# MLP of a two-layer diffusion transformer: layer 1's modulation summed in PSUM, late row sums on GpSimd, and another order of the second stage's first loads and splits

## The chip, the core and the metric

The kernel runs on one core of a Trainium2 chip. The core's engines are TensorE (PE; its weight loads are listed as PEld), VectorE (DVE), ScalarE (ACT), GpSimd (POOL) and SyncE (SP), which here issues the DMA transfers. SBUF is the working memory, PSUM the eight banks into which PE writes products. The metric is the device time of one execution in microseconds (us).

## The reference

Two layers, each an adaptive norm, a token mixer and an MLP, over 1024 tokens of 1024 channels; layer 0 also carries 256 context tokens. What matters here is the MLP and the modulation that scales its input:

```python
mod_l = (jax.nn.silu(c) @ ada_w[layer] + ada_b[layer]).reshape(batch, 1, N_MOD, D_MODEL)
mod_c = (jax.nn.silu(c_ctx) @ ada_w[layer] + ada_b[layer]).reshape(1, 1, N_MOD, D_MODEL)
...
def modulate(x, g, mod, i):
    return rms_norm(x, g) * (1 + mod[:, :, i + 1]) + mod[:, :, i]

def sq_relu_mlp(h, w1, w2):
    return jnp.square(jax.nn.relu(h @ w1)) @ w2
...
x = x + mod_l[:, :, 5] * sq_relu_mlp(modulate(x, norm2_g[layer], mod_l, 3), mlp_w1[layer], mlp_w2[layer])
```

`w1` is 1024 x 4096, `w2` 4096 x 1024, all in float32. The modulation of a layer is a vector times a 1024 x 6144 matrix, once for the tokens and once for the context.

## The kernel before

**Arithmetic.** A float32 product is made of three TensorE products of a high and a low part. So each operand is split: ACT rounds it to its high part (L389), GpSimd or DVE subtracts that to get the low part (L390).

**The MLP's first stage** (`mlp_hidden`) makes the hidden layer in 16 pairs of 2 x 128 hidden channels, as a seven-product scheme for 2 x 2 blocks. `start` does pairs 0 and 1, `pair` the pairs 2 to 15, each with the products "11", "S1", "12", "S2", "22", "S3", "S4" of 12 matmuls of 128 x 512; in layer 0 two direct products of the context (24 matmuls of 128 x 256 each) stand after "12" and after "S3". Every product takes the next PSUM bank of a ring `A`: in layer 0 after `start` the seven banks 4, 5, 6, 0, 1, 2, 3, in layer 1 all eight. Bank 7 (`N`) takes the small sums of the modulation in layer 0. A bank is emptied ("drained") by ACT (L800 for "11", L592 for the context), by DVE (L635) for the rest. ACT then does relu and square (L592, L593), and the blocks of the hidden layer are stored to DRAM (`hd`, `hc`; L595).

**Sums for the second stage.** For each pair three column sums and two row sums of its hidden blocks are also made on DVE and stored (`kept_sum`, L609 to L611). For pairs 0 and 1, whose blocks are complete too early for that, `late_load` fetches four blocks from DRAM after pairs 7 and 10 (L617), and the "late sums" are made in the next pair.

**Operands.** While pair b runs, the generator `sums(b + 1)` makes the next pair's operands, a step after each product: additions on GpSimd (L553) and splits (ACT L389, GpSimd L390). In pair 15 the generator `ahead` takes that place: it loads (L915), adds (L960) and splits the first operands of the second stage.

**The filler.** In layer 0 the first stage also makes layer 1's modulation (`ada_sums`): 12 blocks of 512 columns, each of eight loads of 128 x 512 (L204) that DVE multiplies, row by row, by the entries of silu(c) and adds to the sum so far (L211 for the first, L213 for the rest); the first four blocks do this for tokens and context ("two streams"), the rest for the tokens alone. PE then adds up over the 128 partitions with tiny matmuls by ones (L222), and DVE adds the bias (L225). `fill` advances this by one step at three places of a pair. The sums lie in SBUF tiles `acc`, of which there is one per stream (512 columns for the tokens, two of 256 for the context).

**The second stage** (`mlp_out`) multiplies the hidden blocks by `w2`; its first products are those of line L1037.

**Order.** PE, DVE, ACT and GpSimd run `start` in program order, and with SP also pairs 14 and 15; elsewhere a scheduler orders each engine's instructions. Every engine's queue runs in order.

Of the kernel before, what the change touches and what calls it, by code (L numbers as in the profile page):

```python
# [14 lines left out]
ALU = mybir.AluOpType  # L15
# [6 lines left out]
ND = D // P  # L22
# [24 lines left out]
PG = 1024  # L47
# [32 lines left out]
def cuts(big, n, *offs):  # L80
    return [big[:, o : o + n] for o in offs]
# [15 lines left out]
class Kernel:  # L97
# [99 lines left out]
    def ada_sums(self, layer, block, streams, tp, psp, tag):  # L197


        nc, a = self.nc, self.a  # L200
        acc = [[tp.tile([P, n], F32, tag=f"acc{v}") for _ in range(512 // n)] for v, n in enumerate((512, 256)[:streams])]
        for k in range(ND):
            w = tp.tile([P, 512], F32, tag="raw")
            nc.sync.dma_start(w, a["ada_w"][layer, k * P : (k + 1) * P, block * 512 : block * 512 + 512])  # L204
            for v in range(streams):
                c = self.cs[:, k, v : v + 1]
                n = 512 // len(acc[v])
                for i, t in enumerate(acc[v]):
                    x = w[:, i * n : i * n + n]
                    if k == 0:  # L210
                        nc.vector.tensor_scalar(t, x, c, None, op0=ALU.mult)  # L211
                    else:
                        nc.vector.scalar_tensor_tensor(t, x, c, t, op0=ALU.mult, op1=ALU.add)  # L213
            if k % 4 == 3:
                yield
        pt = psp.tile(tag, "adapt")
        for v in range(streams):
            n = 4 // len(acc[v])
            for i in range(4):
                o = 8 * v + 2 * i  # L220
                t = acc[v][i // n][:, i % n * P : i % n * P + P]
                nc.tensor.matmul(pt[:, o : o + 2], t, self.ones[:, 0:2], start=True, stop=True)  # L222
        c0 = block * 4
        for v in range(streams):
            nc.vector.tensor_tensor(  # L225
                self.mod[layer][:, c0 : c0 + 4, v], pt[:, 8 * v : 8 * v + 8].rearrange("p (i e) -> p i e", e=2)[:, :, 0],
                self.v(V_AB + layer * 48 + c0, 4), op=ALU.add,
            )
        yield
# [276 lines left out]
    def mlp_hidden(self, layer, groups, hds, begin, slots, tp, feed, filler):  # L506
# [4 lines left out]
        nc, a = self.nc, self.a  # L511
        F, W = self.F, self.W
        ctx = groups[2:]
        c0, c1 = (slice(t0, t0 + n) for t0, n, _ in LGS)
        psp = self.banks(A=(0, 1, 2, 3, 4, 5), N=(7, 6) if ctx else (6, 7))
        parts = [W[i][:, o : o + PG] for i in slots[:5] for o in (PG, 0)]
# [11 lines left out]
        x = self.x  # L528
# [6 lines left out]
        def op(src):  # L535
            o = tp.tile([P, PG], F32R, tag="op")
            o = o[:, :H], o[:, H:]
            self.split(*o, src, nc.gpsimd)
            return o
# [8 lines left out]

        def sums(b, A, w):

            a11, a12, a21, a22 = w
            s = tp.tile([P, H], F32, tag="s")
            add = lambda o, p, q, how: nc.gpsimd.tensor_tensor(o, p, q, op=how)  # L553
            A["11"] = op(a11)
            add(s, a21, a22, ALU.add)
            yield
            A["S1"] = op(s)
            add(s, s, a11, ALU.subtract)
            yield
            A["12"] = op(a12)  # L560
            yield
            A["S2"] = op(s)
            add(a11, a11, a21, ALU.subtract)
            yield
            A["22"] = op(a22)
            add(s, a12, s, ALU.subtract)
            yield
            A["S3"] = op(a11)
            yield
            A["S4"] = op(s)  # L570
            yield
            if ctx:
                A["21"] = op(a21)
            yield
# [12 lines left out]
        def temp(n=512):  # L587
            return tp.tile([P, n], F32, tag="u")
# [8 lines left out]
        def part(b, i):  # L597
            return hd[b][:, i * H : i * H + H]
# [7 lines left out]
            job = lambda: finish(ps, tp.tile([P, CTX], F32, tag=tag), hc[b][:, e * CTX : e * CTX + CTX])  # L606
            job() if later is None else later.append(job)

        def kept_sum(b, i, o, p, q, how=ALU.add):  # L609
            tt(o, p, q, how)  # L610
            nc.sync.dma_start(part(b, i), o)  # L611

        def late_load(b):

            h = [temp() for _ in range(4)]
            for t, i in zip(h, (5, 7, 8, 2)):
                nc.sync.dma_start(t, part(b, i))  # L617

            def late_sums():
                column_sums(b, h[0], h[2], h[3])  # L620
                row_sums(b, h[0], h[1], h[3])

            return late_sums

        def column_sums(b, h11, h21, h22):
            kept_sum(b, 1, temp(), h21, h11, ALU.subtract)
            kept_sum(b, 0, temp(), h11, h22)
            kept_sum(b, 4, h21, h21, h22)

        def row_sums(b, h11, h12, h22):  # L630
            kept_sum(b, 6, temp(), h12, h22, ALU.subtract)
            kept_sum(b, 3, h12, h11, h12)

        def tt(o, p, q, how=ALU.add):
            nc.vector.tensor_tensor(o, p, q, op=how)  # L635
# [150 lines left out]
        def pair(b, A, nxt):  # L786
# [58 lines left out]
            step()  # L845
            step()
            pending["row"] = lambda: row_sums(b, h11, v, h22)

        def ahead():


            at = tp.tags["op"][1]
            w = W[slots[5]]
            tp.place("op", [parts[(at + i) % 10] for i in range(10)] + [w[:, :PG], w[:, PG:]])
            tp.place("raw", cuts(F, PG, 0, PG, 2 * PG))
            tp.place("b", cuts(F, PG, 5 * PG, 6 * PG))
            eng = nc.gpsimd
            if filler:
                yield
                yield  # L860
            for k in range(2):
                feed.load(k)
            feed.load_a(2)
            yield
            feed.split_a(0, eng)
            yield
            feed.split_b(0, eng)
            feed.load_b(2)
            yield
            if not filler:  # L870
                yield
                yield
            for k in (1, 2):
                feed.split_a(k, eng)
                feed.split_b(k, eng)
                yield

        R, pending = {}, {}
        E = mybir.EngineType
# [1 line left out]
        def load(b):  # L881
            if b < NFF // 2 and b not in R:
                R[b] = raws(b)

        A = start()
        for b in range(2, NFF // 2):
            B = {}
            for i in range(1, 2 if ctx else 3):
                load(b + i)
            nxt = sums(b + 1, B, R[b + 1]) if b + 1 < NFF // 2 else ahead()  # L890
            if b < NFF // 2 - 2:
                pair(b, A, nxt)
            else:
                with self.tc.manual_schedule(engines={E.PE, E.DVE, E.Activation, E.Pool, E.SP}):
                    pair(b, A, nxt)
            A = B
            if b in (7, 10, NFF // 2 - 1):
                pending.pop("row")()
                if b < 11:
                    pending["late"] = late_load((b - 7) // 3)  # L900
# [1515 lines left out]
```

## Time and profile before

| | us |
|---|---|
| median of 3 runs | 2829.03 (2823.62 to 2830.92) |
| profiled execution | 2817.14 |
| its span in the trace | 2815.4, mean granted clock 0.989 |
| PE busy | 2711.1 (96%) |
| DVE busy | 1955.4 (69%) |
| ACT busy | 1474.7 (52%) |
| POOL busy | 1116.1 (40%) |
| layer 0's pairs 2 to 15 | 822 to 1229.3 |

The trace is of one execution and has its own time, beside the median of several. A row of waits reads: the engine, what it wrote and its line, what it waited for, then the total in us, the number of waits, and the longest. In a timeline the columns are the start, the length, the engine, line, operation, output <- input, shape and count, and in brackets the idle time before it and what ended it.

### The profile page before, as it was taken

To read this page: it belongs to the slowest core of one execution; us is meant where nothing else is said; L and a number is where in the kernel's file an instruction comes from. 1 tells how busy PE (TensorE), PEld (TensorE's weight loads), DVE (VectorE), ACT (ScalarE), POOL (GpSimd) and SP (SyncE) were. 2 spreads that over 40 slices of the span, in tenths; PEclk is the share of its full clock that TensorE was granted. 3 is DMA by queue.
4 is the path that set the end of the run, shared out by engine and by line. 5 is a ranking of instruction groups with operands and counts; after the bars stand their busy time and mean duration, and the time that the engine had idled before them with its cause. 6 is when DMAs were issued, how large, how long until landed. Compare 5 with 4: busy or idle time off the path is not lost.

```text
span 2815.4 us, 40957 instructions
## 1 busy us (share of the span) xinstructions
PE 2711.1 (96%) x14747; PEld 2299.1 (82%) x14747; DVE 1955.4 (69%) x3300; ACT 1474.7 (52%) x2611; POOL 1116.1 (40%) x740
## 2 busy tenths in 40 slices
PE   6899999999999999989999999999999999999999
PEld 3788888878788787868888889999988888878887
DVE  4646555578877977666777756888884667666776
ACT  4655554544664243434346646888775555444442
POOL 3521121111238565640001345777776398740000
PEclk9999999999999999989999999999999999999999
DMA  7222224442324566578855820000036245478674
GB/s 238 67 78 94 97 100 135 143 161 87 119 85 151 172 223 226 175 243 303 288 191 177 260 79 24 24 20 27 24 110 218 70 165 195 169 260 278 220 235 153
DMA packets 194662, 428.36 MB, mean 152 GB/s; under 512 B 21129, under 2 KB 47337, under 8 KB 194457
## 3 DMA queue, kind: packets, MB, share of 16 engines
q1 hardware_dynamic: 194456, 425.73, 45.4%
q8 instruction: 116, 1.90, 0.3%
q14 instruction: 90, 0.73, 0.1%
HBM read 322.90 MB, written 102.74 MB: 151 GB/s over the span
## 4 chain that ended last, share of the span: by engine, by line
PE 63%; DVE 12%; DMA 8%; issue 4%; ACT 3%; POOL 1%; SPq 0%; DVEq 0%; POOLq 0%; ACTq 0%
PE psum L580 17%; PE psum L1037 12%; DMA hhiraw<-in_w 5%; PE psum L415 4%; PE psum L417 4%; PE psum L416 4%; PE psum L2004 4%; PE psum L2190 3%; PE psum L1133 3%; PE psum L1910 3%; DVE W L390 2%; DVE F L635 1%; DVE F L213 1%; POOL W L390 1%; DMA hd<-F 1%
## 5 line engine op out<-in xcount | busy, mean ns | idle before, releaser
L390 POOL TENSOR_TENSOR W<-F,W 128x512 fp32r<-128x512 f32 (+2 forms) x323 | 518.7, 1621 | 544.0 <-ACT W L389 433.0
L1037 PE MATMUL psum<-W,W 128*128 128x512 f32 x2688 | 616.7, 392 | 13.1 <-POOL W L390 8.0
L1037 PEld LDWEIGHTS psum<-W,W 128*128 128x128 f32 x2688 | 505.8, 189 | 123.7 <-POOL W L390 10.1
L580 PE MATMUL psum<-hhi,W 128*128 128x512 f32 (+1 forms) x1600 | 451.0, 362 | 8.4 <-DVE x L635 6.5
L389 ACT ACTIVATE W<-F 128x512 fp32r<-128x512 f32 (+2 forms) x380 | 273.4, 739 | 261.4 <-POOL F L553 93.8
L580 PEld LDWEIGHTS psum<-hhi,W 128*128 128x128 f32 x1600 | 291.6, 194 | 54.3 <-DVE x L635 5.6
L580 PE MATMUL psum<-hlo,W 128*128 128x512 f32 (+1 forms) x800 | 288.3, 360 | 0.0
L389 ACT ACTIVATE W<-hhiraw 128x1024 fp32r<-128x1024 f32 x98 | 104.0, 1061 | 307.8 <-PE psum L1037 203.4
L415 PE MATMUL psum<-hhi,W 128*128 128x512 f32 (+1 forms) x624 | 232.7, 373 | 0.5 <-ACT F L1422 0.5
L417 PE MATMUL psum<-hhi,W 128*128 128x512 f32 (+1 forms) x624 | 226.6, 363 | 0.0
L416 PE MATMUL psum<-hlo,W 128*128 128x512 f32 (+1 forms) x624 | 226.2, 362 | 0.0
L553 POOL TENSOR_TENSOR F<-F 128x512 f32<-128x512 f32 x112 | 168.7, 1507 | 20.2 <-DMA F<-in_w 10.5
L960 DVE TENSOR_TENSOR hhiraw<-hhiraw 128x512 f32<-128x512 f32 x154 | 106.4, 701 | 96.7 <-DMA hhiraw<-in_w 95.9
L580 PEld LDWEIGHTS psum<-hlo,W 128*128 128x128 f32 x800 | 155.1, 194 | 21.3 <-issue 0.2
L390 DVE TENSOR_TENSOR W<-hhiraw,W 128x1024 fp32r<-128x1024 f32 x98 | 119.7, 1222 | 63.3 <-ACT W L389 62.0
L382 POOL TENSOR_TENSOR hlo<-F,hhi 128x512 fp32r<-128x512 f32 (+1 forms) x24 | 27.4, 1144 | 341.5 <-ACT F L373 341.5
L415 PEld LDWEIGHTS psum<-hhi,W 128*128 128x128 f32 x624 | 118.0, 189 | 20.9 <-ACT x L389 2.5
L416 PEld LDWEIGHTS psum<-hlo,W 128*128 128x128 f32 x624 | 118.1, 189 | 17.1 <-issue 2.2
L417 PEld LDWEIGHTS psum<-hhi,W 128*128 128x128 f32 x624 | 117.9, 189 | 16.7 <-issue 0.2
L592 ACT ACTIVATE F<-F 128x512 f32<-128x512 f32 x82 | 51.3, 626 | 141.5 <-DVE F L635 141.5
L390 DVE TENSOR_TENSOR W<-hloraw,W 128x1024 fp32r<-128x1024 f32 x98 | 121.0, 1234 | 4.1 <-ACT W L389 4.1
L580 PE MATMUL psum<-x,W 128*128 128x512 f32 x504 | 123.5, 390 | 0.0
(442 smaller groups left out, 6363.4 us busy)
## 6 DMA issues: line engine op xcount, KB each, us to landing
F<-in_w SPq DMA_DIRECT2D x104, 512.0 KB
hloraw<-hd SPq DMA_DIRECT2D x90, 512.0 KB
hhiraw<-in_w SPq DMA_DIRECT2D x72, 512.0 KB
hd<-F SPq DMA_DIRECT2D x142, 256.0 KB
hhiraw<-in_w SPq DMA_DIRECT2D x116, 256.0 KB
F<-in_ada_w SPq DMA_DIRECT2D x96, 256.0 KB
hd<-x SPq DMA_DIRECT2D x90, 256.0 KB
F<-in_win SPq DMA_DIRECT2D x33, 512.0 KB
```

Of the source, the lines that this page charges most:

```text
L389: nc.scalar.activation(hi, src, AF.Copy)
L390: eng.tensor_tensor(lo, src, hi.bitcast(F32), op=ALU.subtract)
L415: nc.tensor.matmul(ps, sh, mh, start=i == 0, stop=False)
L416: nc.tensor.matmul(ps, sh, ml, start=False, stop=False)
L417: nc.tensor.matmul(ps, sl, mh, start=False, stop=i == n - 1)
L553: add = lambda o, p, q, how: nc.gpsimd.tensor_tensor(o, p, q, op=how)
L580: nc.tensor.matmul(ps, w[i][:, p], B[j][k], start=first and j == 0 and m == 0, stop=last and j == 3 and m == 2)
L960: tt = lambda o, p, q, how: eng.tensor_tensor(o, p, q, op=how)
L1037: nc.tensor.matmul(bank(base + i), A[u][:, p], B[v], start=first and m == 0, stop=last and m == 2)
L1133: nc.tensor.matmul(bank(k), B[u][:, i * P : i * P + P], A[v][:, half], start=f == 0 and m == 0, stop=f == NFF - 1 and m == 2,)
L1910: nc.tensor.matmul(ps, s[:, c], m[:, j, t0 : t0 + QT], start=j == 0 and i == 0, stop=j == ND - 1 and i == 2)
L2004: nc.tensor.matmul(u.o[:, :QT], v[x], p[y], start=c == 0 and m == 0, stop=c == 2 * NB - 1 and m == 2)
```

## The change

Four things are changed, all in the MLP's code.

The modulation's sums grow in PSUM. `ada_sums` takes a bank for each stream (`X`, `Y`); the first product of a block (now L209) and the six additions behind it (L211) go there, and only the eighth addition (L216) writes to the SBUF tile `acc` that PE reads. In layer 0, after `start`, the ring `A` has the banks 0 to 4, `Y` bank 5, `X` bank 6, `N` bank 7.

The row sums of the late sums run on GpSimd; column sums stay on DVE.

`ahead` has another order in both layers: the first weight load and the second step's weights come first, the splits of step 0 each a step earlier in layer 0, the second step's splits before the third's.

The raw tiles of `ahead` are taken in the order 2PG, 0, PG in place of 0, PG, 2PG.

```diff
@@ ada_sums
+        sums = [psp.tile(t, "adacc") for t in "XY"[:streams]]
         acc = [[tp.tile([P, n], F32, tag=f"acc{v}") for _ in range(512 // n)] for v, n in enumerate((512, 256)[:streams])]
...
-                n = 512 // len(acc[v])
-                for i, t in enumerate(acc[v]):
-                    x = w[:, i * n : i * n + n]
-                    if k == 0:
-                        nc.vector.tensor_scalar(t, x, c, None, op0=ALU.mult)
-                    else:
-                        nc.vector.scalar_tensor_tensor(t, x, c, t, op0=ALU.mult, op1=ALU.add)
+                if k == 0:
+                    nc.vector.tensor_scalar(sums[v], w, c, None, op0=ALU.mult)
+                elif k < ND - 1:
+                    nc.vector.scalar_tensor_tensor(sums[v], w, c, sums[v], op0=ALU.mult, op1=ALU.add)
+                else:
+                    n = 512 // len(acc[v])
+                    for i, t in enumerate(acc[v]):
+                        x = slice(i * n, i * n + n)
+                        nc.vector.scalar_tensor_tensor(t, w[:, x], c, sums[v][:, x], op0=ALU.mult, op1=ALU.add)
@@ mlp_hidden
-        def kept_sum(b, i, o, p, q, how=ALU.add):
-            tt(o, p, q, how)
+        def kept_sum(b, i, o, p, q, how=ALU.add, eng=nc.vector):
+            eng.tensor_tensor(o, p, q, op=how)
...
-                row_sums(b, h[0], h[1], h[3])
+                row_sums(b, h[0], h[1], h[3], nc.gpsimd)
...
-        def row_sums(b, h11, h12, h22):
-            kept_sum(b, 6, temp(), h12, h22, ALU.subtract)
-            kept_sum(b, 3, h12, h11, h12)
+        def row_sums(b, h11, h12, h22, eng=nc.vector):
+            kept_sum(b, 6, temp(), h12, h22, ALU.subtract, eng)
+            kept_sum(b, 3, h12, h11, h12, ALU.add, eng)
@@ ahead
-            tp.place("raw", cuts(F, PG, 0, PG, 2 * PG))
+            tp.place("raw", cuts(F, PG, 2 * PG, 0, PG))
...
-            if filler:
-                yield
-                yield
-            for k in range(2):
-                feed.load(k)
+            feed.load(0)
+            feed.load_a(1)
+            yield
+            feed.split_a(0, eng)
+            yield
+            feed.split_b(0, eng)
             feed.load_a(2)
             yield
-            feed.split_a(0, eng)
-            yield
-            feed.split_b(0, eng)
+            feed.load_b(1)
+            feed.split_a(1, eng)
+            yield
             feed.load_b(2)
             yield
-            if not filler:
-                yield
-                yield
-            for k in (1, 2):
-                feed.split_a(k, eng)
-                feed.split_b(k, eng)
-                yield
+            feed.split_b(1, eng)
+            yield
+            feed.split_a(2, eng)
+            feed.split_b(2, eng)
+            yield
@@ before the loop over the pairs 2 to 15
+        if ctx:
+            psp.tags.update(self.banks(A=(0, 1, 2, 3, 4), N=(7,), X=(6,), Y=(5,)).tags)
```

How the instructions stand, at three places. The first is DVE at the bias addition of the modulation's first block (L225, now L228), in a pair early in layer 0's first stage; `cs` holds silu(c), the `F` and `x_` tiles without psum are SBUF. Before:

```order
L225 TENSOR_TENSOR mod_83<-psum,vec 128x4 x2
L211 TENSOR_SCALAR F<-F,cs 128x512
L211 TENSOR_SCALAR x_7126<-F,cs 128x256
L211 TENSOR_SCALAR x_7127<-F,cs 128x256
L213 SCALAR_TENSOR_TENSOR F<-F,cs 128x512
L213 SCALAR_TENSOR_TENSOR x_7126<-F,cs,x_7126 128x256
L213 SCALAR_TENSOR_TENSOR x_7127<-F,cs,x_7127 128x256
```

The same place of the changed kernel:

```order
L228 TENSOR_TENSOR mod_83<-psum,vec 128x4 x2
L216 SCALAR_TENSOR_TENSOR F<-F,cs,psum 128x512
L216 SCALAR_TENSOR_TENSOR x_7126<-F,cs,psum 128x256
L216 SCALAR_TENSOR_TENSOR x_7127<-F,cs,psum 128x256
L209 TENSOR_SCALAR psum<-F,cs 128x512 x2
L211 SCALAR_TENSOR_TENSOR psum<-F,cs,psum 128x512 x3
L638 TENSOR_TENSOR x_7126<-psum,x_7126 128x512
```

Before, the second block's sum begins behind the first block's bias addition; in the changed order the second block's last step stands there, and behind it the third block begins.

The second place is SP near the end of layer 0's first stage, where the second stage's first loads stand (L915, now L919; `in_w` is `w2`, `hd_0` pair 0's hidden blocks). Before, from the last sums of pair 14 on:

```order
L611 DMA hd_14_6492<-x_7127 128x512 x3
L1110 DMA x_10153<-xs_116 128x512
L1110 DMA x_10154<-xs_116 128x512
L1110 DMA x_10155<-xs_116 128x512
L1110 DMA x_10153<-xs_116 128x512
L595 DMA hd_15_6493<-x_7127 128x512
L595 DMA hc_15_6509<-F 128x256
L915 DMA F<-in_w 128x512 x2
L915 DMA F<-hd_0_6478 128x1024
L915 DMA F<-in_w 128x512 x2
L915 DMA F<-hd_1_6479 128x1024
```

The changed kernel has the first `L919 DMA F<-in_w 128x512 x2` among the stores of pair 13 and goes on like this from the sums of pair 14:

```order
L919 DMA F<-hd_0_6478 128x1024
L919 DMA F<-in_w 128x512 x2
L614 DMA hd_14_6492<-x_7127 128x512 x2
L1114 DMA x_10125<-xs_116 128x512
L1114 DMA x_10126<-xs_116 128x512
L1114 DMA x_10127<-xs_116 128x512
L1114 DMA x_10129<-xs_116 128x512
L1114 DMA x_10130<-xs_116 128x512
L598 DMA hd_15_6493<-x_7127 128x512
L598 DMA hc_15_6509<-F 128x256
L919 DMA F<-in_w 128x512 x2
L919 DMA F<-hd_1_6479 128x1024
```

Step 0's loads and step 1's weights have moved ahead of pair 15's stores; the hidden tiles of steps 1 and 2 still stand behind the first of them (step 2's comes right after the last row). The loads of L1114 are tiles of `x` for the second stage's end.

The third place is GpSimd there: the last pair's additions (L553, now L556), and the second stage's (L960, now L964). Before:

```order
L553 TENSOR_TENSOR F<-F 128x512
L390 TENSOR_TENSOR W_4597<-F,W_4597 128x512
L553 TENSOR_TENSOR F<-F 128x512
L390 TENSOR_TENSOR W_4597<-F,W_4597 128x512
L390 TENSOR_TENSOR W_4594<-F,W_4594 128x512 x2
L960 TENSOR_TENSOR F<-F 128x512
L390 TENSOR_TENSOR W_4596<-F,W_4596 128x1024
```

Now:

```order
L964 TENSOR_TENSOR F<-F 128x512
L393 TENSOR_TENSOR W_105<-F,W_105 128x512
L556 TENSOR_TENSOR F<-F 128x512
L393 TENSOR_TENSOR W_105<-F,W_105 128x512
L556 TENSOR_TENSOR F<-F 128x512
L393 TENSOR_TENSOR W_106<-F,W_106 128x512 x2
L556 TENSOR_TENSOR F<-F 128x512
L393 TENSOR_TENSOR W_4597<-F,W_4597 128x512
L556 TENSOR_TENSOR F<-F 128x512
L393 TENSOR_TENSOR W_4596<-F,W_4596 128x1024
L393 TENSOR_TENSOR W_4597<-F,W_4597 128x512
L393 TENSOR_TENSOR W_4594<-F,W_4594 128x512 x2
```

The second stage's first addition stands ahead of all the last pair's operands, and the split of its first weights (W_4596, 128x1024) ahead of that pair's last three.

More of the change, by code (lines that the diff above doesn't have):

```diff
@@ L854, in ahead @@
             tp.place("op", [parts[(at + i) % 10] for i in range(10)] + [w[:, :PG], w[:, PG:]])
-            tp.place("raw", cuts(F, PG, 0, PG, 2 * PG))
+            tp.place("raw", cuts(F, PG, 2 * PG, 0, PG))
             tp.place("b", cuts(F, PG, 5 * PG, 6 * PG))
             eng = nc.gpsimd
-            if filler:
-                yield
-                yield
-            for k in range(2):
-                feed.load(k)
-            feed.load_a(2)
+            feed.load(0)
+            feed.load_a(1)
             yield
@@ L867, in ahead @@
             feed.split_b(0, eng)
+            feed.load_a(2)
+            yield
+            feed.load_b(1)
+            feed.split_a(1, eng)
+            yield
             feed.load_b(2)
             yield
-            if not filler:
-                yield
-                yield
-            for k in (1, 2):
-                feed.split_a(k, eng)
-                feed.split_b(k, eng)
-                yield
+            feed.split_b(1, eng)
[3 more added lines that the diff above has]
+            yield
         R, pending = {}, {}
```

## The prediction

> **What bounds the kernel now.** I read the chain of waits first, by engine, then the waits inside layer 0's first MLP stage (822 to 1229 us, where the modulation's sums run beside it), then windows and single waits of that stage, and last the two places where a second stage begins.
>
> ```profile
> PE 63%; DVE 12%; DMA 8%; issue 4%; ACT 3%; POOL 1%; SPq 0%; DVEq 0%; POOLq 0%; ACTq 0%
> 822.00:1229.30 407.30, 392.19 (x2094) 340.27 (x2092) 315.48 (x387) 158.53 (x308) 251.22 (x169) 0.97 0.55 181
> 1015.00:1041.00 26.00, 26.00 (x142) 22.28 (x141) 21.98 (x24) 8.68 (x16) 16.89 (x12) 1.00 0.70 233
> ```
>
> TensorE (PE) holds most of the chain. The windows give us, busy us of PE, weight load, DVE, ACT and POOL, then PE's granted clock. In this stage PE is busy for 392.2 of 407.3 us at a mean clock of 0.97. At full clock the work is 392.2 x 0.97 = 380 us, as the third row shows it is done where nothing is late (26 us of work in 26 us, clock 1.00). So at most 407.3 - 380 = 27 us can be won in the stage. Where they are lost:
>
> ```profile
> PE psum L222 <- DVE F L213: 7.7, 4, 3.7
> PE psum L580 <- DVE x L635: 6.5, 4, 3.1
> PE psum L580 <- ACT F L800: 1.0, 1, 1.0
> DVE x L635 <- PE psum L580: 4.0, 1, 4.0
> ACT F L592 <- DVE F L635: 104.6, 21, 12.2
> POOL W L390 <- ACT W L389: 133.4, 39, 11.7
> 924.05 1.05 PE L222 MATMUL psum<-ones,F 128*128 128x2 f32 x8 [1.14 <-DVE F L213]
> 985.29 1.05 PE L222 MATMUL psum<-ones,F 128*128 128x2 f32 x8 [3.75 <-DVE F L213]
> 1208.44 1.87 PE L222 MATMUL psum<-ones,F 128*128 128x2 f32 x8 [2.11 <-DVE F L213]
> 901.00:933.00 32.00, 30.86 (x153) 27.06 (x152) 27.75 (x38) 10.41 (x21) 17.04 (x12) 0.89 0.49 164
> 963.00:1015.00 52.00, 48.26 (x242) 41.85 (x241) 43.69 (x63) 18.48 (x37) 30.96 (x21) 0.93 0.61 201
> 1210.10:1215.30 5.20, 5.20 (x25) 5.20 (x26) 2.84 (x5) 5.14 (x11) 1.73 (x2) 0.51 0.48 176
> 1100.00:1130.00 30.00, 25.75 (x132) 21.53 (x131) 24.00 (x28) 11.08 (x21) 17.96 (x13) 0.94 0.72 241
> ```
>
> PE waits four times, 7.7 us, for the last modulation sum (L213) before the tiny matmuls that reduce it (L222); and five times, 7.5 us, for a drain that must empty a PSUM bank. DVE waits for a product only once: it runs behind PE, not PE behind it. ACT waits 104.6 us for DVE here, and POOL 133.4 us for ACT. After the waits for L213 the clock is low: 0.89 over 32 us, 0.93 over 52, 0.51 over 5.2.
>
> **The sums in PSUM.** Twelve blocks, four of them with two streams. Durations (busy us, mean ns):
>
> ```profile
> L213 DVE SCALAR_TENSOR_TENSOR F<-F,cs 128x512 f32<-128x512 f32 x84 | 94.9, 1129 | 8.8 <-DMA F<-in_ada_w 7.6
> L213 DVE SCALAR_TENSOR_TENSOR x<-F,cs,x 128x256 f32<-128x256 f32 x56 | 43.0, 805 | 0.0
> L211 DVE TENSOR_SCALAR F<-F,cs 128x512 f32<-128x512 f32 x12 | 13.7, 1145 | 4.7 <-DMA F<-in_ada_w 4.7
> L211 DVE TENSOR_SCALAR x<-F,cs 128x256 f32<-128x256 f32 x8 | 6.3, 829 | 0.0
> L635 DVE TENSOR_TENSOR F<-psum,F 128x512 f32<-128x512 f32 x49 | 32.5, 680 | 3.5 <-DMA hd<-F 3.4
> L635 DVE TENSOR_TENSOR F<-F 128x512 f32<-128x512 f32 x15 | 17.5, 1167 | 5.0 <-DMA hd<-F 2.8 <-ACT F L593 2.1
> L1760 DVE SCALAR_TENSOR_TENSOR x<-psum,mod,x 128x512 f32<-128x512 f32 x48 | 35.7, 746 | 26.1 <-PE psum L417 16.8 <-PE psum L2190 5.1 <-DMA x<-xd 2.9
> L330 DVE TENSOR_TENSOR psum<-psum,F 128x512 f32<-128x512 f32 x36 | 25.0, 695 | 14.2 <-ACT F L328 13.7
> ```
>
> Removed: 94.9 + 43.0 + 13.7 + 6.3 = 157.9 us of DVE. In this same stage an addition with one input in PSUM takes 680 ns and one with both in SBUF 1167. The new form (one input SBUF, one PSUM) has no row; nearest is L1760, 746 ns, and for a first product written into PSUM L330, 695. Added: 12 x 7 + 4 x 6 = 108 long sums x 0.746 = 80.6; 16 first products x 0.695 = 11.1; the 8 half-width last sums at their old 0.805 = 6.4. Together 98.1, so DVE loses 60 us of its 315. Bounds: if the new form were held up like the old, 108 x 1.129 + 16 x 1.145 + 6.4 = 146.7, a saving of 11; the low end is the 680 of the drains, a saving of 67. I take 746, the row of the same operation with the same mixture of inputs.
>
> The row of 680 against 1167 ns is also where the Trainium skill speaks, page "SBUF — State Buffer", section "Who interferes with whom": a VectorE instruction with at most one SBUF input does not contend with GpSimd, one with two does. By that rule the sum stays at 98; the trace agrees as far as its drains go.
>
> What this buys on PE is the release. Before, the sum grows in the tile that L222 reads, so all eight steps of a block stand between two groups of L222. Now only the last step, three instructions at most, writes that tile, and it stands right behind the previous block's bias addition (the two lists of DVE's order in the part on the change): those are 3 x 0.75 us after a release that comes a pair ahead of the next L222. The four waits go, **-7.7 us**, and the slow clock behind them: 0.11 x 32 = 3.5, 0.07 x 52 = 3.6, 0.49 x 5.2 = 2.5, **-9.6**. Bounds -10 (the clock stays slow for another reason) to -17.3; I take all, since each slow window begins at such a wait.
>
> **The ring of banks, 7 to 5.** A bank now has to be empty four products after its own, not six. In a pair in which all runs well:
>
> ```profile
> 1047.67 0.84 PE L580 MATMUL psum<-W,W 128*128 128x512 f32 x3
> 1048.45 0.58 ACT L800 ACTIVATE F<-psum 128x512 f32<-128x512 f32 x1
> 1051.64 1.27 DVE L635 TENSOR_TENSOR F<-psum,F 128x512 f32<-128x512 f32 x2
> 1054.45 6.77 DVE L213 SCALAR_TENSOR_TENSOR F<-F,cs 128x512 f32<-128x512 f32 x4
> 1061.14 1.27 DVE L635 TENSOR_TENSOR F<-psum,F 128x512 f32<-128x512 f32 x2
> ```
>
> "22" (from 1047.67) would need the bank that ACT empties until 1049.03: 1.4 us late. The product after it needs the drain that ends at about 1052.3; PE, pushed back to 1051.8, waits 0.5. The next pair's first product (1058.7, then 1060.6) needs the drain of "S2", ended at 1062.4: 1.8. Together 3.7 us a pair if the drains stay as late. But what makes the last late is the 6.77 us of four L213; four of the new kind take 3.0. The relief per pair is 60/14 = 4.3 us plus what the late row sums free. I let this and today's waits (7.5, and 0.06 x 30 = 1.8 of clock) cancel: **0**, bounds -9 (all waits go) to +52 (14 pairs x 3.7).
>
> **The late row sums on GpSimd.** Four instructions a layer:
>
> ```profile
> L553 POOL TENSOR_TENSOR F<-F 128x512 f32<-128x512 f32 x112 | 168.7, 1507 | 20.2 <-DMA F<-in_w 10.5 <-PE psum L580 3.0
> ```
>
> 4 x 1.5 = 6 us more for POOL, 4 x 1.17 = 4.7 less for DVE in each layer. Behind each on POOL stand the next pair's additions and splits, which PE needs a pair later; POOL sits idle 133.4 us of this stage and lies on 1% of the chain. Their stores stand on SP ahead of the next modulation loads, so these start up to 3 us later. **0**; without the cover it is 12 us over both layers.
>
> **The second stage's start.** Rows of both places:
>
> ```profile
> 1229.30:1262.00 32.70, 24.78 (x93) 19.23 (x93) 18.40 (x14) 15.95 (x20) 19.41 (x9) 0.84 0.81 286
> 1262.00:1290.00 28.00, 28.00 (x125) 23.21 (x124) 18.12 (x20) 10.29 (x11) 0.00 (x0) 1.00 1.04 394
> 1232.37 0.80 PE L1037 MATMUL psum<-W,W 128*128 128x512 f32 x1 [3.05 <-ACT W L389]
> 1236.62 6.91 PE L1037 MATMUL psum<-W,W 128*128 128x512 f32 x17 [3.46 <-POOL W L390]
> 1224.50 0.90 SPq L915 DMA_DIRECT2D F<-in_w  x2
> 1229.02 1.26 POOL L960 TENSOR_TENSOR F<-F 128x512 f32<-128x512 f32 x1 [11.63 <-DMA F<-in_w]
> L389 ACT ACTIVATE W<-F 128x1024 fp32r<-128x1024 f32 x6 | 6.0, 1050 | 14.0 <-POOL F L960 14.0
> L390 POOL TENSOR_TENSOR W<-F,W 128x1024 fp32r<-128x1024 f32 x6 | 15.0, 2528 | 3.5 <-ACT W L389 3.5
> 2506.75 23.57 PE L1037 MATMUL psum<-W,W 128*128 128x512 f32 x102 [3.15 <-POOL W L390]
> ```
>
> 93 matmuls take 32.7 us where the next 125 take 28.0, so 20.8 would do: 11.9 us are lost, because POOL waits until 1229.02 for a weight load that SP issues at 1224.50, when the hidden stage has ended. The new order issues the first two weight loads in pairs 13 and 14 and the first hidden tile in pair 14, and POOL's first second-stage addition stands ahead of the last pair's operands. The two splits of step 0 are done before 1229. Still late is step 1's hidden tile: its load stands on SP behind a store of the last pair, as step 0's did, so it lands at about 1228; with 1.06 of ACT and 2.5 of POOL it is ready near 1232, while step 0, whose 18 matmuls are recorded here in two rows, feeds PE until about 1229.3 + 18 x 0.224 = 1233.3. Leaving 3 us for a late store or a slow clock: **-9**, bounds 0 and -11.9. In layer 1 the loads came ahead already and only the splits of steps 1 and 2 were late, 3.15 us: **-2**, bounds 0 and -3.15. POOL's longer split ahead of two operands of pair 15 (2.45 us) is covered by its 11.63 us of idling.
>
> **Sum.** -7.7 - 9.6 + 0 + 0 - 9 - 2 = -28. The profiled execution took 2817.14 us (span 2815.4) and lies 11.9 below the median of 2829.03, inside what the runs spread. The losses are taken off the median: **2801**.
>
> **Rivals.** (1) The five banks decide: if ACT's copy and DVE's drains keep their lags, every pair pays 3.7 us, 14 pairs 52; less 7.7 + 9 + 2 and, the waits keeping the clock uneven, nothing else: 2829 + 52 - 19 = 2862 in full, about **2845** if half the pairs are hit or relieved by half. It decides as soon as DVE saves less than about 2 us a pair ahead of "S2"'s drain. For it: DVE runs behind PE today. Against: the saving is 4.3, and much of the lag is the very group of L213 that shrinks.
>
> The Trainium skill, page "TensorE: Matmul & The Clock Gate", section "A second HAM failure mode: psum-queue depth-cycling", goes further: short idling of PE between groups while it cycles through banks makes the clock oscillate. The 1.14 us wait at 924 with 0.89 behind it bears that out; at 3.5 us more a pair it would put this rival near 2890.
>
> (2) The start of the second stage gains nothing, since its loads or POOL's splits are as late as before behind the last pair's stores: 2829 - 17 = **2812**. For it: step 1's tile is still behind such a store. (3) The PSUM form is held up like the SBUF one (1129 ns): DVE saves 11 us instead of 60, bank waits and their clock double, +9: **2810**. Against: no drain with a PSUM input in the stage is slow. (4) The waits only change their name: PE stands at a bank where it stood at L222, the stage keeps its 27 us, and half of the rest comes: **2824**.
>
> **Chances.** Forecast 0.58, (1) 0.14, (2) 0.12, (3) 0.09, (4) 0.07. A measurement of this kernel tells about 0.3% (8.5 us) from no change. Faster: 0.56 of the forecast, 0.10 of (2), 0.06 of (3): 0.72. Same: 0.02 + 0.02 + 0.03 + 0.07 = 0.14. Slower: (1), 0.14. Range: low is all losses won, 27 + 11.9 + 3.15 = 42, 2787; high takes in (2) to (4) and a mild form of (1) (17 won, 20 lost): 2832. The forecast's own range is 2787 to 2813.
>
> **What would show it.** Right: no wait of L222 for a sum, the new sums near 0.75 us, the stage near 388 us at clock 0.99, the first 93 matmuls of L1037 in under 25 us. Wrong: "PE psum L580" waiting for DVE or ACT by more than 10 us in the stage, a clock below 0.97, or POOL's split still ending the wait at the second stage.

## The result, and the profile after

The changed kernel takes 2798.57 us (median of 4 runs, 2797.2 to 2800.02) against 2828.91 before (4 runs, 2823.62 to 2830.92): a ratio of 0.9898, 95% interval 0.9887 to 0.991, so 30.3 us less. The forecast was 2801.

The profiled executions differ by less: spans 2815.4 and 2797.6 us, 17.8. The missing part lies ahead of the change. I use one mark that both kernels have, the first matmul of product "S2" in pair 2 (L580 before, L583 after, the first with `W` as an input): it starts at 849.3 us before and at 858.9 after, though no work ahead of it was changed, and in a second profile of the same changed kernel at 852.6. So the first 850 us scatter by some ten us from one execution to the next, and stages are compared from that mark on. Windows of both kernels, from the mark to the first second-stage matmul (L1037, now L1041), and from there to layer 1's mixer (columns as in the prediction). Before:

```profile
849.30:1232.40 383.10, 364.93 (x1919) 315.25 (x1917) 288.87 (x357) 145.26 (x281) 236.58 (x160) 0.97 0.58 191
1232.40:1547.90 315.50, 310.11 (x1347) 254.64 (x1348) 230.00 (x251) 144.64 (x171) 30.16 (x15) 0.98 0.73 246
```

After:

```profile
858.90:1213.30 354.40, 351.83 (x1919) 305.81 (x1918) 224.64 (x319) 147.62 (x278) 223.15 (x163) 1.00 0.61 204
1213.30:1528.80 315.50, 309.75 (x1348) 253.30 (x1347) 228.86 (x252) 144.79 (x171) 24.69 (x13) 0.99 0.73 246
```

All of the 28.7 us between the marks are in the first stretch, and PE is now busy for 351.8 of its 354.4 us at full clock. The second stretch has not moved. Of the 28.7 us, 13.1 are PE's shorter busy time for the same matmuls (364.93 to 351.83, at a clock of 0.97 and of 1.00), and 15.6 are idle time of PE that is gone: 7.7 ahead of the tiny matmuls, 4.9 at banks, 3.05 ahead of the first second-stage matmul. The modulation's sums after (busy us, mean ns, idle before), and all waits of PE from 822 to 1260 us:

```profile
L211 DVE SCALAR_TENSOR_TENSOR psum<-F,cs,psum 128x512 f32<-128x512 f32 x96 | 70.6, 751 | 33.9 <-DMA F<-in_ada_w 33.4
L209 DVE TENSOR_SCALAR psum<-F,cs 128x512 f32<-128x512 f32 x16 | 11.7, 750 | 4.8 <-DMA F<-in_ada_w 4.7
L216 DVE SCALAR_TENSOR_TENSOR F<-F,cs,psum 128x512 f32<-128x512 f32 x12 | 8.9, 739 | 1.4 <-DMA F<-in_ada_w 1.4
L216 DVE SCALAR_TENSOR_TENSOR x<-F,cs,psum 128x256 f32<-128x256 f32 x8 | 3.5, 476 | 0.0
...
PE psum L1041 <- ACT W L392: 2.9, 1, 2.9
PE psum L1041 <- POOL W L393: 1.6, 1, 1.6
PE psum L583 <- DVE F L638: 1.6, 1, 1.6
PE psum L583 <- DVE x L638: 1.0, 2, 0.8
PE psum L583 <- ACT F L595: 0.8, 1, 0.8
```

The sums take 94.7 us in place of 157.9, and DVE now waits 39.5 us for their loads (L209, L211, L216), which it did for 12 before. No matmul of L225 waits any more, and the waits for a bank have fallen from 7.5 us to 3.4 (2.6 between the marks). What is left of PE's waiting is the start of the second stage.

### The profile page after: what moved, and what is told of

It is laid out like the page before. It is cut to its first block, busy times and chain, and to the rows that moved or that the text cites. A ratio compares the mean times of both kernels' runs of the same rounds, so it can differ in the third digit from the quotient of the medians.

```text
span 2797.6 us, 40915 instructions
## 1 busy us (share of the span) xinstructions
PE 2704.7 (97%) x14747; PEld 2293.1 (82%) x14747; DVE 1886.7 (67%) x3264; ACT 1478.2 (53%) x2611; POOL 1104.2 (39%) x748
## 4 chain that ended last, share of the span: by engine, by line
PE 70%; DVE 8%; DMA 5%; issue 3%; ACT 2%; POOL 1%; DVEq 0%; SPq 0%; POOLq 0%; ACTq 0%
PE psum L583 22%; PE psum L1041 13%; PE psum L418 4%; PE psum L419 4%; PE psum L420 4%; PE psum L2008 4%; DMA hhiraw<-in_w 4%; PE psum L2194 4%; PE psum L1137 3%; PE psum L1914 3%; DVE W L393 2%; DVE x L1046 1%; POOL W L393 1%; PE psum L1494 1%; PE psum L2070 1%
## 5 line engine op out<-in xcount | busy, mean ns | idle before, releaser
L393 POOL TENSOR_TENSOR W<-F,W 128x512 fp32r<-128x512 f32 (+2 forms) x323 | 498.8, 1558 | 541.7 <-ACT W L392 427.4
L1041 PE MATMUL psum<-W,W 128*128 128x512 f32 x2688 | 617.0, 391 | 9.8 <-DVE W L393 4.1
L1041 PEld LDWEIGHTS psum<-W,W 128*128 128x128 f32 x2688 | 504.2, 188 | 122.2 <-DVE W L393 9.4
L583 PE MATMUL psum<-hhi,W 128*128 128x512 f32 (+1 forms) x1600 | 442.4, 356 | 2.7 <-DVE x L638 1.0
L583 PEld LDWEIGHTS psum<-hhi,W 128*128 128x128 f32 x1600 | 285.1, 189 | 47.0 <-issue 2.8
L583 PE MATMUL psum<-hlo,W 128*128 128x512 f32 (+1 forms) x800 | 284.3, 355 | 0.0
L964 DVE TENSOR_TENSOR hhiraw<-hhiraw 128x512 f32<-128x512 f32 x154 | 107.9, 709 | 106.6 <-DMA hhiraw<-in_w 105.6
L556 POOL TENSOR_TENSOR F<-F 128x512 f32<-128x512 f32 x112 | 164.7, 1470 | 13.3 <-DMA F<-in_w 4.3
L583 PEld LDWEIGHTS psum<-hlo,W 128*128 128x128 f32 x800 | 151.2, 189 | 21.4 <-issue 0.2
L583 PE MATMUL psum<-x,W 128*128 128x512 f32 x504 | 123.5, 389 | 0.0
L1914 PE MATMUL psum<-hhi,W 128*128 128x256 f32 x512 | 111.7, 292 | 0.7 <-DVE F L1827 0.7
```

The costliest lines, as they stand in the source:

```text
L393: eng.tensor_tensor(lo, src, hi.bitcast(F32), op=ALU.subtract)
L583: nc.tensor.matmul(ps, w[i][:, p], B[j][k], start=first and j == 0 and m == 0, stop=last and j == 3 and m == 2)
L964: tt = lambda o, p, q, how: eng.tensor_tensor(o, p, q, op=how)
L1041: nc.tensor.matmul(bank(base + i), A[u][:, p], B[v], start=first and m == 0, stop=last and m == 2)
L1914: nc.tensor.matmul(ps, s[:, c], m[:, j, t0 : t0 + QT], start=j == 0 and i == 0, stop=j == ND - 1 and i == 2)
```

## The experiments

Times are medians, ratios against the kernel before run beside them.

**The parts alone.** Three kernels are the kernel before with one part of the change, a fourth has the ring's cut without the sums.

`sums_alone`: `ada_sums` of the changed kernel and its ring.

```diff
+        if ctx:
+            psp.tags.update(self.banks(A=(0, 1, 2, 3, 4), N=(7,), X=(6,), Y=(5,)).tags)
```

> The kernel before with the first part of the change alone: the modulation's sums grow in PSUM and the ring has five banks. The prediction's steps give -17 us (four waits of L222 and the slow clock behind them, nothing from the ring): 2812. The traces of before and after, in which the stage is 26 us shorter, give -26: 2803, with the drains early enough for five banks. A rival in which the late row sums on GpSimd are needed to make room on VectorE gives less than half of that, 2816 or more.

Measured: 2800.39 us, ratio 0.9903 (0.9888 to 0.9918), 26.4 less than before. The stretch to the second stage takes 357.2 us. So this part carries nearly all of the gain, and more than the 17 us that the prediction gave it.

`five_banks`: the kernel before with five banks, its sums in SBUF.

```diff
+        if ctx:
+            psp.tags.update(self.banks(A=(0, 1, 2, 3, 4), N=(7,)).tags)
```

> The kernel before with the ring of banks cut from seven to five after the first two pairs and nothing else: what the ring costs while the sums still grow in SBUF. By the lags of the pair read for the prediction (3.7 us a pair) +52 us: 2881; if only half the pairs have such lags +26: 2855; if the lags of that pair were the exception, under +10. In each case the added idle time of TensorE is in waits for a drain.

Measured: 2824.12 us, ratio 0.999 (0.9981 to 0.9999): no loss at all. The window of its stretch, and PE's waits from 822 us to the end of the stretch, but for the one at its end:

```profile
854.60:1234.90 380.30, 361.80 (x1918) 311.57 (x1916) 288.77 (x356) 145.36 (x279) 232.64 (x159) 0.98 0.58 191
PE psum L580 <- DVE x L635: 10.6, 6, 3.7
PE psum L580 <- DVE F L635: 2.7, 2, 2.1
PE psum L580 <- ACT F L592: 1.7, 2, 1.3
PE psum L580 <- ACT x L592: 0.5, 1, 0.5
PE psum L580 <- ACT F L800: 0.4, 1, 0.4
```

The waits for banks have doubled to 15.9 us, but the waits of L222 for the sums are gone, though each sum still stands as late in DVE's order (DVE's instructions are the same, one by one). Before, the two kinds added up to 15.2 us. PE waits for a late DVE either at a bank or at L222; the ring only chooses the place. So, by these sums, the lag of 3.7 us "a pair" and the four waits "for the release" were one lateness counted at two places. Nor does every pair pay its lag anew: 14 pairs of 3.7 us would be 52 us, and the waits grew by 8.4 at the banks and fell by 7.7 at L222.

`ahead_alone`: `ahead` of the changed kernel.

> The kernel before with the new order of the second stage's first loads and splits alone. The prediction's step gives -9 in layer 0 and -2 in layer 1: 2818. The trace of after shows some -3 and 0: 2826. If the new order's gain needs a VectorE that is on time, as a rival reading says, 0: 2829.

Measured: 2824.55 us, ratio 0.9991 (0.9982 to 1.0001), 2.3 us less, which isn't clearly apart from nothing. In its trace the stretch behind the first second-stage matmul takes 317.0 us (315.5 before).

`rows_alone`: the late row sums on GpSimd.

```diff
-                row_sums(b, h[0], h[1], h[3])
+                row_sums(b, h[0], h[1], h[3], nc.gpsimd)
```

> The kernel before with the late row sums on GpSimd alone. The prediction has 0 (6 us more for GpSimd in each layer, hidden; 4.7 us less for VectorE): 2829 within 3. If VectorE's lateness is what the stage pays for, up to -5: 2824. If GpSimd's later operands are paid for, +6 to +12.

Measured: 2830.26 us, ratio 1.0011 (1.0001 to 1.0021). The stretch of the stage takes 382.8 us (383.1 before), so the trace shows no place in it for the 3.5 us; layer 1's first stage takes 952.7 us in its trace and 951.7 before.

`rows_back`: the changed kernel with that part taken back.

> The changed kernel with the late row sums on VectorE as before, which leaves the sums in PSUM and the new order. The prediction has 0 for this part: 2798 to 2800. By the run of that part alone (3.5 us slower, interval 0.3 to 6) it is a loss: 2795.

Measured: 2794.64 us, ratio 0.9888 (0.9873 to 0.9903), beside 0.9898 (0.9887 to 0.991) of the changed kernel. The two runs point to a small loss; the last run below does not. What the row sums cost is within 4 us of nothing, and its sign is not settled.

**Why the sums gain: release, VectorE's time, or its meeting with GpSimd.** `tied` lets a block's first step write the SBUF tile that PE reads, so that the whole block stands behind its release again:

```diff
-                if k == 0:
-                    nc.vector.tensor_scalar(sums[v], w, c, None, op0=ALU.mult)
...
+                    if k == 0:
+                        nc.vector.tensor_scalar(t, w[:, x], c, None, op0=ALU.mult)
+                    elif k == 1:
+                        nc.vector.scalar_tensor_tensor(sums[v][:, x], w[:, x], c, t, op0=ALU.mult, op1=ALU.add)
...
```

> The changed kernel, in which the first product of each block goes to the SBUF tile that TensorE reads, and the second step takes it from there: so all eight steps of a block stand behind the release of that tile again, as before, while six of eight stay in PSUM. VectorE gets some 15 to 20 us more of work. Theory of the release (the prediction's step: the four waits of L222 and the clock behind them): the stage returns to some 370 us or more and the time to 2815. Theory of the backlog (the time that VectorE's work takes is what TensorE waits for, wherever it stands): the stage stays near 357, the time near 2800 to 2803.

Measured: 2808.53 us, ratio 0.9931 (0.9914 to 0.9947); the stretch takes 362.7 us. Between the two forecasts. Its window, PE's waits for banks from 822 us on, and the two forms whose inputs all lie in SBUF:

```profile
855.10:1217.80 362.70, 354.92 (x1917) 308.22 (x1917) 249.72 (x329) 145.83 (x278) 230.38 (x164) 0.99 0.60 200
PE psum L585 <- DVE x L640: 7.2, 4, 3.2
PE psum L585 <- ACT F L597: 1.3, 1, 1.3
PE psum L585 <- ACT x L597: 0.6, 1, 0.6
...
L214 DVE SCALAR_TENSOR_TENSOR psum<-F,cs 128x512 f32<-128x512 f32 x12 | 19.8, 1654 | 0.2
L212 DVE TENSOR_SCALAR F<-F,cs 128x512 f32<-128x512 f32 x12 | 14.4, 1202 | 5.9 <-DMA F<-in_ada_w 5.9
```

Again no wait at the tiny matmuls: with the release as before, PE is held by drains, and the operation with two inputs in SBUF takes 1654 ns where the one with an input in PSUM takes 751. The loss against the changed kernel, some 8 us of the stretch and 10 of the medians, is the release and 25 us more of VectorE's work (249.7 against 224.6) together; this run can't part them. So the release is worth 8 of the 28.7 us at most, unless something else in this kernel makes up for it.

`busy` gives VectorE work in SBUF:

```diff
+            nc.vector.tensor_scalar(w[:, :256], w[:, :256], 1.0, None, op0=ALU.mult)
```

> The changed kernel, with VectorE made as busy as before in the stage: after each of the 96 loads it also multiplies half of the loaded tile by 1 in place (128 x 256, both ends in SBUF, so it meets GpSimd as the old sums did), some 60 to 80 us. The release stays as in the changed kernel. Theory of the release: the stage stays near 355 to 360, the time near 2800. Theory of the backlog: the stage returns to some 380 us, the time to 2822 or more, with the idle time of TensorE in waits for drains.

Measured: 2814.83 us, ratio 0.9957 (0.9942 to 0.9972); the stretch is 376.7 us long, so 22 of the 28.7 us are lost again with the release untouched (16 us of the medians), and PE waits 17.3 us for drains (the three rows of waits below). This looked like the backlog, until `busy_psum` gave VectorE as much work in PSUM (the same line stands ahead of a block's last step too):

```diff
+                    if v == 0:
+                        nc.vector.tensor_scalar(sums[v], sums[v], 1.0, None, op0=ALU.mult)
```

> The changed kernel with 84 multiplications by 1 of the sum in place in PSUM (128 x 512), some 58 us more for VectorE that touch no SBUF, so GpSimd isn't held up by them. If VectorE's time alone is what the stage pays for, the stage returns to 375 us or more, as in the run with the multiplications in SBUF, and the time to 2815. If it was the meeting of VectorE and GpSimd at SBUF, the stage stays below 362 and the time near 2800.

Measured: 2794.46 us, ratio 0.9886 (0.9871 to 0.9902): nothing lost. Windows of the stretch, first `busy`, with PE's longest waits for banks and two rows of its added work, one with DVE's wait ahead of it, one with its shortest, median and longest:

```profile
853.00:1229.70 376.70, 359.30 (x1918) 309.98 (x1918) 274.42 (x414) 146.04 (x278) 226.43 (x164) 0.98 0.59 195
PE psum L584 <- DVE x L639: 10.3, 3, 4.8
PE psum L584 <- ACT F L804: 4.5, 2, 2.7
PE psum L584 <- DVE F L639: 2.5, 3, 1.4
L206 DVE TENSOR_SCALAR F<-F 128x256 f32<-128x256 f32 x96 | 54.7, 579 | 37.8 <-DMA F<-in_ada_w 37.4
L206 DVE TENSOR_SCALAR F<-F x96: 275/295/1387, 827.0 to 1203.3; 128x256 f32<-128x256 f32 x96
```

and `busy_psum`:

```profile
855.50:1207.70 352.20, 351.36 (x1918) 305.92 (x1918) 277.09 (x403) 147.41 (x278) 224.87 (x164) 1.00 0.63 208
L212 DVE TENSOR_SCALAR psum<-psum 128x512 f32<-128x512 f32 x72 | 49.9, 693 | 1.3
L213 DVE SCALAR_TENSOR_TENSOR psum<-F,cs,psum 128x512 f32<-128x512 f32 x96 | 70.4, 747 | 6.7 <-DMA F<-in_ada_w 5.6
```

DVE is busy for 274 and 277 us of the stretch, yet one takes 377 us and the other 352. So VectorE's time as such is not what the stage pays for, and the theory of the backlog, in the form in which I had put it, falls. Two things differ. In `busy` the work meets GpSimd in SBUF: the same instruction takes 275 to 1387 ns, in the mean 288 where no GpSimd instruction runs at the same time (47 of the 96) and 858 where one does (49). And in `busy` it can't begin before the load has landed, and delays everything behind it, while in `busy_psum` it mostly runs in the time in which DVE would wait for the load anyway (5.6 us of such waiting are left, of 33.4). The runs do not part these two.

**How close the ring is.** `four_banks` is the changed kernel with one bank less.

```diff
-            psp.tags.update(self.banks(A=(0, 1, 2, 3, 4), N=(7,), X=(6,), Y=(5,)).tags)
+            psp.tags.update(self.banks(A=(0, 1, 2, 3), N=(7,), X=(6,), Y=(5,)).tags)
```

> The changed kernel with a ring of four banks in place of five (one bank unused). By the lags that the prediction counted in each pair, four banks would cost more than 3.7 us a pair, 2850 or more. If a late drain is paid once and then worked off, and VectorE now has time left, under 10 us: 2800 to 2808.

Measured: 2801.37 us, ratio 0.9909 (0.9894 to 0.9924).

```profile
853.40:1219.70 366.30, 354.75 (x1918) 307.55 (x1917) 226.18 (x321) 152.62 (x285) 227.11 (x164) 0.99 0.61 201
1219.70:1529.20 309.50, 307.46 (x1347) 252.21 (x1348) 225.50 (x251) 141.30 (x165) 22.04 (x11) 1.00 0.73 246
PE psum L583 <- DVE F L638: 4.8, 1, 4.8
PE psum L583 <- DVE x L638: 4.7, 3, 2.2
```

The first stage loses 12 us, and half of it comes back in the second: PE arrives later at the second stage and finds its operands ready (309.5 us for the stretch that took 315.5).

**The second stage's start.** After the change DVE sits idle at the start of pair 15, and SP shows why:

```profile
1197.62 0.32 SPq L919 DMA_DIRECT2D F<-hd  x1
1197.98 0.91 SPq L919 DMA_DIRECT2D F<-in_w  x2
1198.98 1.21 SPq L614 DMA_DIRECT2D hd<-x  x2
1200.28 3.44 SPq L1114 DMA_DIRECT2D x<-xs  x5
...
1206.74 1.89 DVE L638 TENSOR_TENSOR x<-psum,x 128x512 f32<-128x512 f32 x3 [6.84 <-DMA hd<-x]
1207.47 0.63 ACT L595 ACTIVATE x<-x 128x512 f32<-128x512 f32 x1 [11.81 <-DVE x L638]
1209.39 1.04 ACT L392 ACTIVATE W<-F 128x1024 fp32r<-128x1024 f32 x1
1213.28 3.12 PE L1041 MATMUL psum<-W,W 128*128 128x512 f32 x12
1219.32 0.80 PE L1041 MATMUL psum<-W,W 128*128 128x512 f32 x1 [2.93 <-ACT W L392]
1221.75 28.63 PE L1041 MATMUL psum<-W,W 128*128 128x512 f32 x118 [1.63 <-POOL W L393]
```

The stores of pair 14's row sums (1198.98) stand behind the hidden tile and the second step's weights, and share the queue with five loads of x. Until they land, the tile that the next drain needs isn't free: 6.84 us. ACT, in order, finishes that product before it splits step 0's hidden tile (1209.39), and step 1's splits come behind that.

`stores_first` issues the hidden tile and the second step's weights one step later:

```diff
-            feed.load(0)
+            feed.load_a(0)
+            yield
+            feed.load_b(0)
             feed.load_a(1)
-            yield
             feed.split_a(0, eng)
```

> The changed kernel, with the second stage's first hidden tile and the second step's weights loaded one step later, behind the stores of pair 14's row sums. The trace of after has VectorE waiting 6.8 us at the start of pair 15 for such a store, which stands on SP behind 1 MB of those loads and ahead of five loads of x. If that wait is what makes the first splits late, the matmuls of the second stage start without a gap and the time falls by 3 to 5 us, to 2794. If ACT's own order (finishing the last products ahead of the splits) holds them, under 1 us: 2798.

Measured: 2791.14 us, ratio 0.9876 (0.9862 to 0.9891), the lowest median of all versions, though its interval still touches that of the changed kernel (0.9887 to 0.991). The scheduler also moved four of the five loads of x, and one later weight load, so more than those two loads changed place.

```profile
853.00:1207.00 354.00, 351.58 (x1918) 305.90 (x1917) 224.66 (x319) 150.06 (x282) 225.34 (x164) 1.00 0.61 206
1207.00:1518.30 311.30, 307.51 (x1347) 252.07 (x1346) 226.84 (x252) 142.29 (x168) 22.59 (x12) 1.00 0.72 246
1196.63 1.89 DVE L638 TENSOR_TENSOR x<-psum,x 128x512 f32<-128x512 f32 x3 [2.21 <-DMA hd<-x]
1212.10 28.19 PE L1042 MATMUL psum<-W,W 128*128 128x512 f32 x123 [1.73 <-POOL W L393]
```

DVE's wait fell from 6.84 to 2.21 us, PE's two waits (4.6 us) to one of 1.73, and the stretch behind the first second-stage matmul from 315.5 to 311.3 (314.5 in the changed kernel's second profile, below). That is the size expected of the store, at the place expected; that the two loads alone made it, and not the other loads that moved, is not shown.

`after_again` is the changed kernel once more, beside the next one.

> The changed kernel once more, unchanged, beside the next two: 2798 to 2800 as in its first runs. Its second profile shows whether the first 859 us, in which nothing was changed, differ from one execution to the next as they do from kernel to kernel (849 to 859 so far): if that is chance, they will not be 859 again.

Measured: 2798.02 us, ratio 0.9897 (0.988 to 0.9915); the mark at 852.6 us, the two stretches 356.2 and 314.5. The first 850 us do scatter by chance.

`stores_first_rows_back` has both edits.

> The changed kernel with the hidden tile loaded behind the row sums' stores and the late row sums on VectorE. If the late row sums on GpSimd cost 3.5 us, as their two runs say, 2788; if those were the scatter of the measurement, 2791 as with the loads alone.

Measured: 2794.91 us (2789.41 to 2798.48), ratio 0.9883 (0.9868 to 0.9899), so no faster than `stores_first`: the loss that `rows_alone` and `rows_back` hinted at did not show a third time. In its trace the two stretches are 352.4 and 309.7 us, together the shortest of all, but the difference from `stores_first` is inside the scatter of the medians.

## Why the prediction was right, point by point

- **What the stage could give**: at most 27 us, from busy time and clock. Between the marks it gave 28.7, 3 of them the wait ahead of the first second-stage matmul. PE at 351.8 of 354.4 us has no more to give.
- **The sums' durations**: forecast 0.746 us a step, 98 us in all; measured 0.751 and 94.7. The row of the same operation with one input in PSUM was the right one to take, and the bound of 147 was never near.
- **The four waits and the clock behind them, -17.3**: they went. But the step that names the cause, "what this buys on PE is the release", failed. With the sums in SBUF and five banks the waits of L222 went as well and nothing was won; with the release as before (`tied`) they went too, and the stage lost only 8 of 28.7 us. They were where a late DVE was felt first. What makes DVE late enough to cost the 28.7 us is open between the two differences that `busy` and `busy_psum` leave.
- **The ring, 0 between -9 and +52**: between the marks the banks' waits fell from 7.5 to 2.6 us, so this term was -4.9, and with the clock more: PE's busy time fell by 13.1 us, where the prediction had 9.6 of clock. The upper bound was wrong in kind: 3.7 us of lag in one pair is not 3.7 us in each, as `five_banks` (-2.7 us in all) showed.
- **The late row sums, 0**: not told apart from 0, within 4 us either way.
- **The second stage's start, -9 and -2**: this is the term that was mis-sized. Before, PE waited four times in layer 0 (3.05, 3.46, 1.11 and 0.31, together 7.9 us). The first wait went; of the other 4.9 us, 4.6 stayed. The failing step is that step 0's 18 matmuls feed PE "until about" 1233.3: only 12 of step 0's come ahead of the first that needs step 1 (the row of PE shows 12 ahead of the wait). And step 1, expected "ready near 1232", which was 2.7 us after the hidden stage's end, was ready 8.5 us after it (1213.28 to 1221.75). The prediction had left 3 us for "a late store or a slow clock", but thought of a store ahead of step 1's load; here the loads moved ahead in SP's order delay the stores behind them, a drain waits for the store, and ACT's order hands that on to the splits. In `stores_first` the 8.5 us are 5.1 (1207.00 to 1212.10), so 2.4 us over the forecast remain, whose cause was not tested. In layer 1 PE's wait fell from 3.15 to 1.09 us, the 2 us forecast, but the time behind that point didn't fall in these two profiles (315.8 and 315.9 us) and scatters from 316 to 321 in the others, so that gain is not shown in time.

The sum of -28 was met because the stage gave 8 us more and the second stage's start 8 us less than forecast: two misses of one size that cancelled, which is luck. Of the signs named ahead, the waits of L222, the sums and the banks' waits came out as hoped, but POOL's split still ends a wait at the second stage (1.63 us), which was to mean that the prediction is wrong, and the first 93 matmuls of L1041 take 28.5 us and not under 25 (23.5 in `stores_first`). The rivals: (1) did not come, and four banks still don't bring it (its 2845 was off in any case: with half of the 52 us its own sum gives 2836); (2) came as far as layer 0's later waits go; (3) didn't; (4) is what `five_banks` does, not what the change does.

The Trainium skill, page "SBUF — State Buffer", section "Who interferes with whom", says that a VectorE instruction with at most one SBUF input, outside the two-port modes, doesn't contend with GpSimd, that one with two SBUF inputs contends with a GpSimd instruction that reads SBUF, and that `tensor_scalar`, the instruction added in `busy`, can enter a two-port mode. The traces agree: the sum of 128 x 512 with two SBUF inputs takes 1417 ns in the mean where a GpSimd instruction runs at the same time and 746 where none does (1129 over all; 1654 in `tied`), and with one input in PSUM 751 either way. So the old sums are long where GpSimd is at work. That it is this by which the stage got shorter is favoured by `busy` and `busy_psum`, but not shown.

## What to carry to other kernels

A wait shows where lateness is felt, not what makes it: before a wait is priced, ask where the same lateness would be felt if that wait were taken away, and don't multiply a lag by the number of loops. An engine's busy time alone doesn't tell what its work costs: 58 us more in PSUM, ahead of the waits for loads, cost nothing, and 55 us more in SBUF, behind them, cost 22; which of the two differences matters was not tested. A load that is moved ahead in a queue can delay the stores it has passed, and a store frees a buffer that somebody may wait for.

## What was not expected of the hardware

58 us of VectorE's work in and out of PSUM (49.9 in the 72 of the row above, the rest in 12 more, 0.693 us each) cost nothing beside matmuls that write other banks: PE was busy at full clock for 351.4 of 352.2 us. And a multiplication of 128 x 256 in SBUF beside GpSimd took from 275 to 1387 ns, a factor of five for one and the same instruction; without GpSimd at work it never took more than 297.

Nor did more waiting at banks lower the mean clock here. The Trainium skill, page "TensorE: Matmul & The Clock Gate", section "A second HAM failure mode: psum-queue depth-cycling", describes a kernel in which short idling of PE between groups of matmuls, as it cycles through banks, makes the clock oscillate. Here the clock did fall behind single waits (0.51 from 959.6 to 963.0 us in `five_banks`, behind a wait of 3.7), but with five banks and 15.9 us of waits at them the stretch ran at a mean clock of 0.98 (0.97 with seven banks and 7.5 us), with four banks and the sums in PSUM at 0.99.
